# A limit on how far gathers run ahead that starts at three pairs and rises to eight

## The chip, the cores and the metric

The kernel runs on one core of one Trainium2 chip. The metric is the device time of a whole execution in microseconds (us), the median of several. The runs fell on at least three chips of the same type, and these do not behave alike. On two of them, numbers 13 and 5, the kernel before takes about 405 us; on chip 11 it takes about 358 us. Every comparison below is on one chip, beside runs of the kernel before on that chip, and within one call with one exception: of the eight runs of before that stand beside e9 to e12, seven are those of the call of e5 to e8, on the same chip. The first comparison of before and after has no chip number; it behaves like chip 13.

## The reference, cut to what matters

```python
B, S, N, D = (16, 4096, 2048, 512)
def reference(x, indices, w):
    gathered = x[np.arange(B)[:, None], indices, :].copy()   # B x N rows of 512 floats
    cs = np.cumsum(gathered, axis=1)
    return np.matmul(cs, w).astype(np.float32)
```

The rows to gather are sorted within a sequence, the running sum goes over the 2,048 gathered rows of each of 16 sequences, and the product with `w` makes 64 MB of output.

## The kernel before

Work goes in tiles of 128 rows, and two tiles make a pair `g`; there are 256 tiles and 128 pairs. GpSimd gathers a tile with an indirect DMA into one of eight pair buffers. TensorE (PE) sums a pair with matmuls against a triangular matrix (`sums`), VectorE adds the last column of the pair before (`carry`), PE multiplies by `w` (`project`), ScalarE copies the result out (`drain`) and SyncE's queue stores it. All order between engines is by hand-placed semaphores; `pool.need(s_a, n)` makes GpSimd wait until the sums of `n` pairs are done.

```python
NG = 16                                   # gather buffers in tiles: 8 pairs
NA = 2; NB = 2; NC = 4; NO = 8; AH = 2    # sums, products, carries, outputs; pairs that sums run ahead
# ... (buffers and semaphores cut)
def gather(t):
    g, r = divmod(t, R)                   # R = 2
    pool.need(s_a, g + 1 - NG // R)       # line 104: pair g waits for the sums of pair g - 8
    # ... (choice of the index column cut)
    nc.gpsimd.indirect_dma_start(out=g16[g % (NG // R)][:, r, :], ...).then_inc(s_g[t % NG], 16)

def sums(t):
    g, r = divmod(t, R)
    pe.need(s_g[t % NG], 16 * (t // NG + 1))
    pe.need(s_d, g - NA + 1)
    # ... four matmuls into pa[g % NA]; after the second tile: then_inc(s_a, 1)

def carry(g):
    dve.need(s_a, g + 1)
    # ... cst[g % NC] = pa[g % NA] + last column of the pair before; then_inc(s_d, 1)

# TensorE's order in the steady state:
for g in range(1, G - AH - 1):
    for j in range(R):
        sums(R * (g + AH) + j)
        project(g, j)
```

So one signal, the count `s_a` of summed pairs, wakes two engines: VectorE to carry, and GpSimd to gather further.

## Time and profile before

| | before |
|---|---|
| time, median of 3 | 404.81 us (404.65 to 404.89) |
| span of the profiled run | 403.2 us |
| busy: PE, weight loads, VectorE, ScalarE, GpSimd | 80, 45, 39, 33, 60% |
| queues' share of the 16 DMA engines: gathers, stores and loads | 58.2%, 44.2% |

No engine is full. The prediction below shows the table of windows, the queues and the start. One more reading: the timeline around 201 us, with start, length, engine, operation, and in brackets how long the engine had been idle and what released it.

```profile
201.26 0.39 PE L128 MATMUL pa<-ut,g 128*128 128x128 f16 x4
...
201.86 0.94 POOL L111 DMA_INDIRECT g<-in_x_dram,idxg  x1 [0.30 <-issue]
...
204.22 2.55 DVE L146 TENSOR_TENSOR cst<-pa,cst 128x1024 f16<-128x1024 f32 x2 [3.70 <-PE pa L128]
204.33 1.01 ACT L168 COPY ob<-pb 128x1024 f32<-128x1024 f32 x1 [3.11 <-remote]
204.46 0.94 POOL L111 DMA_INDIRECT g<-in_x_dram,idxg  x1 [1.66 <-PE pa L128]
```

The reader is to see one event. PE finishes the sums of a pair at 201.26 + 0.39 = 201.65 us. VectorE, which has been idle, starts the carry of that pair only at 204.22 us, 2.57 us later, and then does two pairs in one go. ScalarE, VectorE and GpSimd all wake within 0.24 us of each other. GpSimd's burst of gathers had ended at 201.86 + 0.94 = 202.80 us. I call this a **late signal**. It comes once in three pairs, about 1.4 us after a burst of six gathers: five starts 1.24 us apart, the last gather's 0.94 and GpSimd's pause of 1.66 us make 8.8 us, the period of three pairs.

### The profile page before, as it was taken

What the parts mean: (1) busy time and instruction counts of PE and PEld (TensorE: products, weight loads), DVE (VectorE), ACT (ScalarE), POOL (GpSimd) and SP (SyncE); (2) the same over time, 40 slices, a digit from 0 to 9 for tenths busy, and PEclk for the clock granted to TensorE, in tenths of its full rate; (3) what the DMA queues carried; (4) which work ended last, traced back from release to release, by engine and by line L of the source; (5) the groups of instructions that cost most, each with busy time, mean ns of one, the idle gap of its engine ahead of it and who ended that gap; (6) DMA issues with size and microseconds to landing.
All of it is one profiled execution on the core that took longest, in us unless ns stands there. A gap on an engine that the chain in (4) does not pass through costs nothing.

```text
span 403.2 us, 5096 instructions
## 1 busy us (share of the span) xinstructions
PE 324.4 (80%) x2064; PEld 182.4 (45%) x2064; DVE 159.2 (39%) x136; ACT 131.8 (33%) x132; POOL 241.6 (60%) x264
## 2 busy tenths in 40 slices
PE   5617988878888887888888788888878888888893
PEld 2303544444444444444444444444444444444451
DVE  2212443344444334434333443443344343433541
ACT  2102433333334333343333433343333333333442
POOL 6774666566666656666665666666566666666100
PEclk9867999999999999999999999999999999999998
DMA  7996999999999999999999999999999999999954
GB/s 175 140 128 111 278 262 262 280 272 270 259 283 257 272 269 269 279 255 284 256 275 264 278 268 266 277 258 271 267 278 271 257 284 264 277 251 281 287 227 191
DMA packets 56871, 102.32 MB, mean 254 GB/s; under 512 B 6800, under 2 KB 39824, under 8 KB 56848
## 3 DMA queue, kind: packets, MB, share of 16 engines
q0 software_dynamic: 36864, 33.57, 58.2%
q1 hardware_dynamic: 19712, 68.43, 44.2%
q8 instruction: 16, 0.26, 0.3%
q10 hardware_dynamic: 272, 0.00, 0.0%
q14 instruction: 7, 0.06, 0.0%
HBM read 68.42 MB, written 67.11 MB: 336 GB/s over the span
## 4 chain that ended last, share of the span: by engine, by line
PE 79%; issue 15%; DVE 2%; DMA 2%; ACT 0%; SPq 0%; ACTq 0%
PE pb L156 58%; PE pa L128 22%; DVE cst L146 2%; DMA g<-in_x_dram,idx_first 1%; DMA idx_first<-in_indices_dram 0%; ACT ob L168 0%; ACT ob L180 0%; ACTq L23 0%; SPq L332 0%; SPq L78 0%
## 5 line engine op out<-in xcount | busy, mean ns | idle before, releaser
L156 PE MATMUL pb<-w,cst 128*128 128x512 f16 x1024 | 266.7, 384 | 67.9 <-issue 56.6
L111 POOL DMA_INDIRECT g<-in_x_dram,idxg x252 | 236.4, 938 | 132.0 <-PE pa L128 66.3
L146 DVE TENSOR_TENSOR cst<-pa,cst 128x1024 f16<-128x1024 f32 x112 | 137.2, 1225 | 203.2 <-PE pa L128 144.8
L168 ACT COPY ob<-pb 128x1024 f32<-128x1024 f32 x127 | 128.5, 1012 | 261.9 <-remote 132.1
L156 PEld LDWEIGHTS pb<-w,cst 128*128 128x128 f16 x1024 | 94.1, 99 | 141.4 <-issue 65.8
L128 PE MATMUL pa<-ut,g 128*128 128x256 f16 (+1 forms) x1024 | 127.7, 248 | 4.3 <-DMA g<-in_x_dram,idx_first 2.7
L128 PEld LDWEIGHTS pa<-ut,g 128*128 128x128 f16 x1024 | 89.8, 99 | 69.4 <-issue 7.8
L142 DVE CAST cst<-pa 128x1024 f16<-128x1024 f32 x16 | 19.5, 1222 | 25.6 <-PE pa L128 18.4
L244 PE MATMUL pb<-zeros 128*128 128x512 f16 x14 | 5.2, 535 | 1.5 <-DVE zeros L248 1.5
L111 POOL DMA_INDIRECT g<-in_x_dram,idx_first x4 | 3.9, 986 | 2.0 <-DMA idx_first<-in_indices_dram 1.1
L244 PEld LDWEIGHTS pb<-zeros 128*128 128x128 f16 x14 | 1.7, 131 | 3.8 <-issue 1.9
L302 ACT CAST w<-w 128x512 f16<-128x512 f32 x2 | 1.2, 618 | 2.8 <-DMA w<-in_w_dram 2.8
L265 DVE CAST w<-w 128x512 f16<-128x512 f32 x2 | 0.9, 452 | 3.1 <-DMA w<-in_w_dram 3.1
L251 DVE CAST idxf<-idx 128x128 f32<-128x128 uint32 x2 | 0.5, 238 | 3.5 <-DMA idx<-in_indices_dram 3.5
L299 ACT ACT_TABLE_LOAD x1 | 1.3, 1283 | 1.5 <-SPq L78 1.5
L180 DVE COPY ob<-pb 128x512 f32<-128x512 f32 x1 | 0.7, 691 | 2.1 <-PE pb L156 2.1
L180 ACT COPY ob<-pb 128x512 f32<-128x512 f32 x1 | 0.6, 586 | 0.7 <-PE pb L156 0.7
L248 DVE MEMSET zeros<- 128x256 uint32 x1 | 0.3, 272 | 1.1 <-SPq L78 1.1
L256 PEld LDWEIGHTS pb<-ident,idxf 128*128 128x128 f32 x2 | 0.4, 187 | 0.6 <-DVE idxf L251 0.3
L262 DVE CAST idxg<-pb 128x128 uint32<-128x128 f32 x2 | 0.5, 292 | 0.2 <-PE pb L256 0.2
L256 PE MATMUL pb<-ident,idxf 128*128 128x128 f32 x2 | 0.5, 303 | 0.0
L215 POOL MEMSET ident<- 128x128 f32 x1 | 0.2, 205 | 0.5 <-SPq L78 0.5
(8 smaller groups left out, 1.6 us busy)
## 6 DMA issues: line engine op xcount, KB each, us to landing
out_dram<-ob SPq DMA_DIRECT2D x127, 512.0 KB
g<-in_x_dram,idxg POOLq DMA_INDIRECT x252
w<-in_w_dram SPq DMA_DIRECT2D x4, 256.0 KB
out_dram<-ob SPq DMA_DIRECT2D x2, 256.0 KB, 2.7
idx<-in_indices_dram SPq DMA_DIRECT2D x2, 128.0 KB, 2.6
g<-in_x_dram,idx_first POOLq DMA_INDIRECT x4
idx_first<-in_indices_dram ACTq DMA_DIRECT2D x1, 2.0 KB, 2.2
idx_first<-in_indices_dram SPq DMA_DIRECT2D x1, 2.0 KB, 2.0
```

The lines of the kernel that those rows point to most:

```text
L111: nc.gpsimd.indirect_dma_start(out=g16[g % (NG // R)][:, r, :], out_offset=None, in_=x_flat, in_offset=bass.IndirectOffsetOnAxis(ap=ap, ax ...
L128: mm = nc.tensor.matmul(out=pa[g % NA][:, c] if r == 0 else pa[g % NA][:, c, :, Q:], lhsT=g16[g % (NG // R)][:, r, c * P : (c + 1) * P], r ...
L142: nc.vector.tensor_copy(out=dst[:], in_=pa[g % NA][:]).then_inc(s_d, 1)
L146: nc.vector.tensor_tensor(out=dst[:], in0=pa[g % NA][:], in1=last.unsqueeze(2).broadcast_to([P, DC, R, P]), op=mybir.AluOpType.add,).then_ ...
L156: mm = nc.tensor.matmul(out=pb[g % NB][:, j], lhsT=cst[g % NC][:, c, j, :], rhs=w16[:, c, :], start=(c == 0), stop=(c == DC - 1),)
L168: nc.scalar.copy(out=ob[g % NO][:], in_=pb[g % NB][:]).then_inc(s_e, 1)
L180: copy(out=ob[g % NO][:, j], in_=pb[g % NB][:, j]).then_inc(s_el[j], 1)
L244: nc.tensor.matmul(out=pb[NB - 1][:, R - 1], lhsT=zeros[:, :P], rhs=zeros[:], start=True, stop=True)
L256: nc.tensor.transpose(out=pb[k % NB][:, 0, :P], in_=idxf[:, k, :], identity=ident[:]).then_inc(s_pt, 1)
L265: nc.vector.tensor_copy(out=w16[:, c, :], in_=w32[:, c, :]).then_inc(s_wc, 1)
L299: nc.scalar.copy(out=spare[:], in_=zeros[:, :1])
L302: nc.scalar.copy(out=w16[:, c, :], in_=w32[:, c, :]).then_inc(s_wc, 1)
```

## The change

The intent is to keep GpSimd from running eight pairs ahead in the start, where VectorE, PE and ScalarE stood still while it did, and to reach the old lead of eight by pair 80.

```diff
     NG = 16
+    EARLY = 3
+    RAMP = 16
     NA = 2
...
     def gather(t):
         g, r = divmod(t, R)
-        pool.need(s_a, g + 1 - NG // R)
+        pool.need(s_a, g + 1 - min(NG // R, EARLY + g // RAMP))
```

Pairs 0 to 15 may run 3 pairs ahead of the sums, pairs 16 to 31 may run 4, and so on to 8 from pair 80. I call this limit the **lead**, and the time from the end of the last gather to the end of the kernel the **tail**.

## The prediction

> **What bounds the kernel now.** I read the page first. TensorE (PE) is 80% busy, no engine is full, but the DMA row of the slices stands at 9 from the seventh slice to the thirty-eighth. Then I cut the span into stretches, because a mean over a start, a steady state and an end says little. This is the table of windows (columns: stretch, its length, busy us of PE, weight loads, VectorE, ScalarE and GpSimd with instruction counts, granted clock, DMA share, GB/s):
>
> ```profile
> 10.00:20.00 10.00, 7.03 (x42) 3.77 (x40) 2.58 (x3) 1.01 (x1) 7.56 (x9) 0.83 0.90 137
> 20.00:30.00 10.00, 1.48 (x4) 0.59 (x5) 1.23 (x1) 0.00 (x0) 7.56 (x9) 0.61 0.91 132
> 30.00:40.00 10.00, 7.42 (x31) 3.57 (x30) 2.58 (x3) 2.02 (x2) 4.25 (x5) 0.70 0.61 109
> 40.00:100.00 60.00, 51.00 (x336) 29.17 (x333) 25.50 (x21) 21.25 (x21) 38.46 (x41) 1.00 1.09 269
> 100.00:376.00 276.00, 230.88 (x1507) 131.63 (x1508) 115.54 (x95) 95.13 (x94) 176.74 (x189) 1.00 1.09 270
> ```
>
> The reader is to see two different kernels here. From 40 to 376 us the DMA share is the same 1.09 in both stretches (1.08 to 1.09 in finer cuts) (above 1 because packets of two queues overlap in time), at 269 GB/s: I take that for its ceiling. From 10 to 40 us it moves half as much, and PE nearly stands still from 20 to 30 us.
>
> Next the DMA part of the page, for what one pair of sequence tiles costs the transfer engines:
>
> ```profile
> q0 software_dynamic: 36864, 33.57, 58.2%
> q1 hardware_dynamic: 19712, 68.43, 44.2%
> ```
>
> Of 403.2 us, 58.2% is 234.7 us of gathers, 1.83 us for each of 128 pairs; 44.2% is 178.2 us, nearly all stores, 1.39 us a pair. Together 3.2 us, and divided by the share of 1.09 that runs, 2.95 us. The chain in order of time has a period of three pairs, which is the same rate:
>
> ```profile
> 204.03 1.47 issue
> 205.50 1.04 PE pb L156 x4
> ...
> 212.84 1.47 issue
> 214.30 1.04 PE pb L156 x4
> ```
>
> 212.84 - 204.03 = 8.81 us for three pairs, 2.94 us each. PE alone would take 2.4 us a pair: in the unbroken parts of the same chain two groups of four projections (0.86 us each) and two groups of four sums (0.44 and 0.22) make one pair. So in the steady state the transfers' full engines and the pace agree, although no instruction is shown waiting for a gather there.
>
> Last, the start, in the timeline and in the waits of 10 to 40 us:
>
> ```profile
> 16.73 1.23 DVE L146 TENSOR_TENSOR cst<-pa,cst 128x1024 f16<-128x1024 f32 x1 [4.78 <-PE pa L128]
> 27.24 1.23 DVE L146 TENSOR_TENSOR cst<-pa,cst 128x1024 f16<-128x1024 f32 x1 [9.29 <-remote]
> 28.52 1.89 PE L156 MATMUL pb<-w,cst 128*128 128x512 f16 x4 [8.74 <-issue]
> 34.37 1.01 ACT L168 COPY ob<-pb 128x1024 f32<-128x1024 f32 x1 [17.28 <-remote]
> 34.55 0.94 POOL L111 DMA_INDIRECT g<-in_x_dram,idxg  x1 [4.05 <-PE pa L128]
> ```
>
> After the carry of the second pair at 16.73, VectorE idles 9.29 us, PE 8.74, and ScalarE 17.28 between the first and the second result. GpSimd meanwhile issues a gather every 1.24 us without a pause from 3.26 to 30.5 us and stops only because it is eight pairs ahead. The sums that the carry at 27.24 waits for are recorded as done by 16.93 us. **What holds their signal back for ten microseconds no view says**; it is not an unlanded gather of that pair, and the long delays stop when GpSimd stops: after the last gather (376 us) no such gap is left in the timeline.
>
> **What the Trainium skill says.** "DMA: Bandwidth & Descriptors", section "Issuing engines are not separate DMA queues", says that transfers of all issuers run on the same 16 DMA engines and interleave; the trace agrees, the two queues together fill 1.08 of them. The same page, "Queues, rings and completion order", says that each engine takes turns between its queues packet by packet, so gathers ahead of need delay a store by their share and not by their whole backlog; no view of the kernel before shows that directly. "Perfetto Trace Analysis", section "DMA Instruction — SWDGE (GPSIMD)", says that the end of such an instruction is the end of descriptor generation; agreed, the first gather is issued at 3.26 and 1.13 us long, but the chain holds 5.82 us until PE can use it. "TensorE: Matmul & The Clock Gate", section "Why this matters for your kernels", says that idle gaps over some 3 us drop the clock; agreed, the clock is 0.61 from 20 to 30 us.
>
> **The change part by part.** Nothing is removed or added in work: 256 gathers of 0.94 us, the same matmuls, copies and stores; the comparison of orders shows only waits on GpSimd, one from the fourth pair on instead of the ninth.
>
> *Start.* Pair 3 may go when pair 0 is summed (10.7 us; it went at 10.91, no change). Pair 4 now waits for the sums of pair 1, about 16.7 us instead of 13.40. Then each pair waits for the sums three pairs back. If the long holdup belongs to the uninterrupted stream of gathers, it goes, and PE can walk on from 20 us. What that is worth is bounded by the transfers: between 10 and 40 us the DMA share lost against 1.08 is (0.18 + 0.17 + 0.47) / 1.08 x 10 = 7.6 us; counted in work, three stores were issued where the steady pace makes ten, 7 x 1.39 = 9.7 us. Against that, the pause of GpSimd between about 13 and 16.7 us leaves the engines partly idle, at most 2 to 3 us. **Estimate for the start: 6 to 9 us less.**
>
> *Pairs 4 to 80, three to seven ahead.* Does a lead of three suffice? From the sums of a pair to those three later: wake 0.3, second gather 1.25, landing as long as the first gather's 5.8, the sums 0.4: 7.8 us, 2.6 us a pair, less than the 2.94 that the transfers take. With the 2.6 us delay that one pair in three shows in the steady state it would be about 8.6 us when shared over the three, still just under 8.8. So 0 to 3 us may be lost in the first sixteen pairs, nothing from four ahead.
>
> *Steady state from pair 80 and end.* Same lead, same full engines: no change. But if PE stays on the heels of the gathers, fewer pairs are left when they end: from 376 us on the share is 0.64, over 27 us, and each pair less in that tail saves about half a microsecond, 0 to 4 us.
>
> Sum: -7.5 + 1 - 2 = about -8.5 to -9.5 us, **395.5 us**.
>
> **The rivals.** (1) *The holdup is not the gathers' doing.* One store and PE's throttled clock are in the same window. For it: signals are late in the steady state too. Then the start is unchanged and gathers only start later: 403 to 406 us. (2) *The lead is too short and PE waits for gathers.* For it: gathers share full engines and then land later than 5.8 us; at 7.5 us the loop is 9.5 us, 0.2 us a pair over sixteen pairs, 3 us, and a late signal now stalls GpSimd and then PE. Against it: the ramp gives a fourth pair after sixteen. Alone +3 to +8 us: 408 to 412. (3) *Hidden anyway:* if transfers are the only limit, a lead changes when bytes move, not how many; then only the lost 7.6 to 9.7 us can come back and 394 is the floor. (4) *The late signals vanish over the whole ramp* and the end shortens: 385 to 390. The ceiling of 1.08 speaks against more.
>
> **Range and chances.** Start repaired, rest the same (half): 393 to 399. Start repaired and a shorter tail (15%): 386 to 392. Little or nothing (28%): 399 to 405. Starved (7%): above 406. The 2% line is 396.7 us, in the midst of the likeliest case. Hence 395.5 us, range 387 to 405; faster 0.52, within 2% 0.42, slower 0.06.
>
> **What the profile after would show.** Right: VectorE's 9.29 and ScalarE's 17.28 us idle times gone, PE's gap of 8.74 us gone, the clock not at 0.61 from 20 to 30 us, five or more stores by 40 us, then 1.08 share and the period of 8.8 us again. GpSimd's wait for PE grows early and costs nothing. Wrong: the same gaps at 17 to 34 us (rival 1), PE or its weight loads waiting for gathers between 20 and 70 us with a DMA share below 1.0 (rival 2), or a period below 8.8 us, which would say that the share of 1.08 was no ceiling and that the gain is larger than told.

## The result, and the profile after

| | before | after |
|---|---|---|
| time, median of 4 | 404.85 us (404.65 to 405.32) | 407.59 us (406.86 to 407.75) |
| span of the profiled run | 403.2 us | 406.0 us |
| end of the last gather | 376.51 us | 379.39 us |
| from there to the end (the tail) | 26.7 us | 26.7 us |

The ratio is 1.0062, with a 95% interval of 1.0045 to 1.008. A ratio here is always the mean time of one kernel's fast runs over that of the other's of the same rounds, so it is not quite the ratio of the medians quoted. The profile after is of its slowest run, 407.75 us. The change is within 2%, on the slow side, and outside the range of the prediction.

The start is repaired as foreseen. This is the table of windows of the kernel after (stretch, its length, busy us and instruction counts of PE, weight loads, VectorE, ScalarE and GpSimd, granted clock, DMA share, GB/s), and below it three lines of its timeline:

```profile
10.00:20.00 10.00, 7.68 (x40) 3.92 (x41) 4.20 (x4) 1.01 (x1) 4.31 (x5) 0.66 0.56 85
20.00:30.00 10.00, 7.05 (x46) 3.57 (x45) 3.44 (x4) 2.86 (x3) 6.29 (x7) 1.00 1.03 214
30.00:40.00 10.00, 8.88 (x59) 4.54 (x57) 4.00 (x4) 3.21 (x4) 6.54 (x8) 1.00 1.04 241
```

```profile
17.32 1.01 ACT L170 COPY ob<-pb 128x1024 f32<-128x1024 f32 x1 [10.37 <-PE pb L158]
17.54 2.55 DVE L148 TENSOR_TENSOR cst<-pa,cst 128x1024 f16<-128x1024 f32 x2 [4.82 <-PE pa L130]
17.78 0.94 POOL L113 DMA_INDIRECT g<-in_x_dram,idxg  x1 [3.87 <-PE pa L130]
```

From 20 to 30 us PE is busy 7.05 us where it was 1.48, at full clock where it was 0.61. ScalarE has 8 copies in these 30 us where it had 3. VectorE's longest idle time here is 4.82 us instead of 9.29. But the first row shows the price: GpSimd is busy only 4.31 us of the ten, and the DMA share is 0.56 at 85 GB/s where the kernel before had 0.90 at 137. The last timeline line tells why: GpSimd stood for 3.87 us, until the signal of PE's sums woke it at 17.78 us.

Now compare how far the engines get by one moment. These are windows of the kernel before, then of the kernel after, cut at 12, 260 and 376 us. An instruction that lies across a cut counts in both rows.

```profile
12.00:260.00 248.00, 200.41 (x1279) 113.39 (x1280) 97.61 (x80) 79.62 (x79) 158.88 (x170) 0.97 1.05 253
260.00:376.00 116.00, 96.88 (x634) 55.12 (x633) 48.45 (x40) 39.80 (x40) 74.15 (x80) 1.00 1.09 270
376.00:406.00 30.00, 20.74 (x130) 11.36 (x128) 9.72 (x9) 9.69 (x10) 0.51 (x1) 0.93 0.58 208
```

```profile
12.00:260.00 248.00, 204.61 (x1268) 111.91 (x1268) 96.45 (x80) 78.09 (x78) 157.39 (x169) 0.96 1.05 250
260.00:376.00 116.00, 97.27 (x635) 55.46 (x636) 48.62 (x40) 40.31 (x40) 75.02 (x80) 1.00 1.09 271
376.00:406.00 30.00, 22.17 (x139) 12.04 (x137) 11.62 (x10) 10.71 (x11) 1.87 (x2) 1.00 0.68 234
```

By 260 us both kernels have done 80 instructions of VectorE, nearly all of them carries, and the kernel after has one gather fewer, 169 against 170. So the start's lead of some 9 us (the carry of pair 20 starts at 73.8 us instead of 82.4, counting VectorE's carries in order) is gone by then. At 376 us the kernel after has ten instructions of VectorE and two gathers left, the kernel before nine and one.

Where it goes is seen at the steps of the ramp. This is the timeline of the kernel after where the lead goes from 4 to 5 (pair 32):

```profile
107.28 1.01 ACT L170 COPY ob<-pb 128x1024 f32<-128x1024 f32 x1 [5.15 <-remote]
107.74 0.94 POOL L113 DMA_INDIRECT g<-in_x_dram,idxg  x1 [0.30 <-issue]
...
110.82 1.23 DVE L148 TENSOR_TENSOR cst<-pa,cst 128x1024 f16<-128x1024 f32 x1 [4.50 <-PE pa L130]
...
111.06 0.93 POOL L113 DMA_INDIRECT g<-in_x_dram,idxg  x1 [2.39 <-PE pa L130]
```

Given one more pair at once, GpSimd issues ten gathers without a pause from 96.55 to 108.68 us, instead of six. The signals in this stretch are later still: ScalarE has been idle 5.15 us before it wakes at 107.28, VectorE 4.50 us before 110.82. Two more rows end the argument, GpSimd's last gather in the kernel before and in the kernel after:

```profile
375.57 0.94 POOL L111 DMA_INDIRECT g<-in_x_dram,idxg  x1 [0.30 <-issue]
```

```profile
378.45 0.94 POOL L113 DMA_INDIRECT g<-in_x_dram,idxg  x1 [0.30 <-issue]
```

The last gather starts 2.88 us later, and the span is longer by as much. What follows the last gather takes the same time in both.

### The profile page after: what moved, and what is told of

It reads as the page before. It is cut to its first block, busy times and chain, and to the rows that moved or that the text cites. A ratio compares the mean times of both kernels' runs of the same rounds, so it can differ in the third digit from the quotient of the medians.

```text
span 406.0 us, 5095 instructions
## 1 busy us (share of the span) xinstructions
PE 331.5 (82%) x2064; PEld 182.3 (45%) x2064; DVE 159.5 (39%) x136; ACT 131.8 (32%) x132; POOL 241.7 (60%) x264
## 4 chain that ended last, share of the span: by engine, by line
PE 71%; issue 13%; DMA 6%; POOL 4%; DVE 3%; another core or an unknown queue 1%; SPq 1%; ACT 0%; ACTq 0%
PE pb L158 51%; PE pa L130 20%; DMA g<-in_x_dram,idxg 5%; POOL g L113 4%; DVE cst L148 2%; DMA w<-in_w_dram 1%; DVE cst L144 1%; DVE w L267 0%; SPq L203 0%; SPq L207 0%; ACT ob L182 0%; SPq L195 0%; SPq L334 0%; ACTq L23 0%
## 5 line engine op out<-in xcount | busy, mean ns | idle before, releaser
L130 PE MATMUL pa<-ut,g 128*128 128x256 f16 (+1 forms) x1024 | 130.3, 250 | 19.4 <-issue 11.3
L130 PEld LDWEIGHTS pa<-ut,g 128*128 128x128 f16 x1024 | 88.8, 99 | 90.8 <-issue 26.5
```

Of the source, the lines that this page charges most:

```text
L130: mm = nc.tensor.matmul(out=pa[g % NA][:, c] if r == 0 else pa[g % NA][:, c, :, Q:], lhsT=g16[g % (NG // R)][:, r, c * P : (c + 1) * P], r ...
```

## The experiments

Theory A, in its final form: **on this chip the stream of gathers keeps one timetable whatever the lead, and the time is the end of that stream plus a tail that grows with the lead.** A smaller lead in the start makes the sums earlier against the same gathers; that is not progress, it is gathers not yet issued, and it is paid back when the lead rises. Only the lead at the end can shorten the kernel. Rival B: the repaired start is a real gain, and the change lost it by something of its own, a lead of three that is too short or a ramp that slows the middle. Rival C: the transfers' full engines are the ceiling, as the prediction took them to be.

A grew. Before e1 to e4 it said "paid back", with rival C's full engines as what sets the pace; the tail of 2.4 us for each pair of lead was read from these four runs, and e13 and e17 are its tests on a slower chip.

All edits are of line 104 unless shown otherwise. Labels that end in "slow" or "third" name the hope for a chip of that kind, not the chip that the run got.

### Constant leads and a quick ramp (one call, chip 13, before 404.99 us)

```diff
-        pool.need(s_a, g + 1 - NG // R)
+        pool.need(s_a, g + 1 - 3)                        # e1_lead3
+        pool.need(s_a, g + 1 - 4)                        # e2_lead4
+        pool.need(s_a, g + 1 - 6)                        # e3_lead6
+        pool.need(s_a, g + 1 - min(NG // R, 3 + g // 2)) # e4_fast_ramp
```

e1_lead3, expected: 

> Lead of 3 pairs to the end, no ramp. Theory (paid back: the transfers' full engines set the pace, the 8.8 us that the changed kernel is ahead at pair 27 are the gathers it has not yet issued, and each step of the ramp pays for one pair of them and loses a little more in a long holdup): with no step nothing is paid back, and the end has five pairs fewer to finish after the last gather; 393 to 399 us, and the sums at pair 77 come 5 us or more before those of the kernel before. Rival (starved: three pairs are too short a lead, TensorE waits for gathers that have not landed): slower than the changed kernel, 412 us or more, with waits for gathers all along and a DMA share below 1.0.

e2_lead4, expected: 

> Lead of 4 pairs to the end. Theory paid back: 394 to 400 us, one pair more to finish at the end than with 3. Rival starved: better than with 3, still no faster than 405 us. Both allow that 4 is better than 3 if 3 starves a little.

e3_lead6, expected: 

> Lead of 6 pairs to the end. Theory paid back: between 4 and 8 pairs, 398 to 403 us, as two pairs fewer are left at the end (some half a microsecond each) and three pairs fewer are gathered in the start. Rival starved: 404 to 405 us, as the kernel before, because six pairs are enough.

e4_fast_ramp, expected: 

> From 3 pairs to 8 within ten pairs of sums. Theory paid back: the lead is paid for in the start, at once and while the engines still have room, with no steps later; 401 to 405 us, the start's gain kept in part. Rival starved: the short lead lasts only for the first pairs, so 404 to 406 us. This run tells the cost of the late steps: about 3 to 6 us less than the changed kernel if the steps cost, the same as the changed kernel if only the start does.

| kernel | time, us | ratio to before (95%) | last gather ends | from there to the end |
|---|---|---|---|---|
| before (lead 8), the first profile | 404.85 | | 376.51 | 26.7 |
| e1, lead 3 | 404.79 median, scattered 401.71 to 413.43 | 0.9996 (0.9955 to 1.0036) | 382.88 | 17.1 |
| e2, lead 4 | 396.07 | 0.9778 (0.9761 to 0.9794) | 377.53 | 17.1 |
| e3, lead 6 | 400.5 | 0.9888 (0.9872 to 0.9905) | 376.96 | 21.9 |
| e4, 3 to 8 by pair 10 | 405.11 | 1.0004 (0.9987 to 1.0021) | 376.76 | 26.7 |

One run of e1, at 413.43 us, was slow (over 1.5% above the kernel's fastest) and is not in its ratio. The times of e2 and e3 lie in the ranges of the theory; that of e1 lies in neither range, and that of e4 in the rival's, just outside the theory's. The two columns on the right are of the profiled runs. The last gather ends at 377 us, give or take 0.6, for leads of 4, 6 and 8, and the tail is 17.1, 21.9 and 26.7 us. That is (26.7 - 17.1) / 4 = 2.4 us for each pair of lead, the pace of PE alone in the prediction's chain: the pairs gathered but not summed when gathering ends are summed afterwards, at PE's own pace (7, 5 and 3 pairs of sums end after the last gather with leads of 8, 6 and 4, most of them 2.39 us apart). The windows of the lead of 4, and its last gather:

```profile
12.00:260.00 248.00, 208.29 (x1343) 117.07 (x1341) 101.36 (x83) 82.99 (x82) 158.54 (x169) 0.99 1.07 261
260.00:376.00 116.00, 96.79 (x630) 54.07 (x628) 48.46 (x40) 40.24 (x40) 73.83 (x79) 1.00 1.09 268
376.00:406.00 30.00, 11.82 (x68) 6.07 (x68) 5.93 (x6) 5.89 (x7) 1.23 (x2) 0.93 0.44 151
```

```profile
376.59 0.94 POOL L111 DMA_INDIRECT g<-in_x_dram,idxg  x1 [0.30 <-issue]
```

By 260 us it has 83 instructions of VectorE, three more than the kernel before, on one gather fewer. After 376 us 6 are left instead of 9. So its sums are three pairs closer to the gathers, and they stay so to the end because the lead never rises.

A lead of three is too short. In the waits of e1 (what waited for what, us in total, times, longest):

```profile
PEld pa L128 <- DMA g<-in_x_dram,idxg: 85.5, 100, 2.3
```

PE's weight loads wait for gathers to land a hundred times, where the same list of the kernel before has one wait for a gather, that for the first pair. The profile is of e1's fastest run, 401.71 us; even there the last gather ends 6.4 us later than that of before, and the tail is no shorter than with four. The late signals are nearly gone in it: by the count described below it has 3 late carries, where the kernel before has 37. So their going does not make this kernel faster, since PE now waits for gathers. This is the part of rival B that holds, for a constant lead of three. The quick ramp is at lead 8 by pair 10, repairs nothing (the carry of pair 3 starts at 34.3 us, as before), and equals the kernel before.

### Ramps at the other end, half stores, a pause between gathers (one call, chip 11, before 357.99 us)

```diff
+        pool.need(s_a, g + 1 - max(4, min(NG // R, 4 + (G - 1 - g) // 8)))   # e5_fall: 8, falling to 4
+        pool.need(s_a, g + 1 - min(NG // R, 4 + max(0, (g - 88) // 8)))      # e6_rise: 4, rising to 8
```
```diff
# e7_half_stores: wrong on purpose, half of the output is not written
-        nc.sync.dma_start(out=dst, in_=ob[g % NO][:]).then_inc(s_o[g % NO], 16)
+        nc.sync.dma_start(out=dst[:, 0], in_=ob[g % NO][:, 0]).then_inc(s_o[g % NO], 16)
# e8_paced: after each gather from the fifth on, 0.2 us of other work for GpSimd (the lines that make pad and s_pad, and the if, cut)
+            pool.need(s_pad, t - FIRST)
+            nc.gpsimd.memset(pad[:], 0.0).then_inc(s_pad, 1)
```

e5_fall, expected: 

> Lead 8 until pair 95, then one pair less every 8 pairs, 4 at the last: the start of the kernel before, the end of lead 4. Theory (the end: from the end of the last gather the kernel needs 7.5 us and 2.39 us for each pair of lead, so 17.1 us at 4 and 26.7 at 8; the last gather is at 377 us in all constant leads because the full engines bring it there): the end shrinks by 9.6 us, but the last gather comes later by the four stores that must now be out before it, 4 x 1.39 = 5.6 us: about 401 us, last gather at 382, tail 17. Rival (it is the start alone that makes lead 4 faster, by the holdup of 17 us that it avoids): 405 us, nothing gained at the end.

e6_rise, expected: 

> Lead 4 until pair 95, then one pair more every 8 pairs, 8 at the last: the start of lead 4, the end of the kernel before. Theory: 27 us from the last gather to the end again, so the 9 us of lead 4 are lost for the most part: 402 to 406 us, the sums at pair 84 still 9 us ahead of the kernel before and at pair 119 no more than 3. Rival (start alone): 396 to 398 us.

e7_half_stores, expected: 

> Kernel before, each store writes one of its two rows per partition: half of the result is missing on purpose, the arithmetic is whole. Theory (full transfer engines set the pace of 2.93 us a pair): stores cost 0.7 us a pair instead of 1.39, so 2.5 us a pair by share, 2.3 in time, below the 2.49 that GpSimd needs to issue two gathers: 2.5 us a pair, 345 to 360 us. Rival (late signals of TensorE are tied to gathers issued without pause and set the pace by themselves): the period stays near 8.8 us for three pairs, 400 to 405 us.

e8_paced, expected: 

> Kernel before with a 0.2 us memset on GpSimd after each gather, so that gathers no longer come without pause. If uninterrupted gathers cause the late signals: the 2.57 us waits of VectorE become fewer or shorter and the 17 us of ScalarE in the start shrink; if full engines set the pace, the time is the same within 1% all the same (402 to 408 us), the last gather near 377 us and 27 us from there. If the signals themselves set the pace, it gets faster with them gone: below 395 us. If GpSimd is slowed so far that it becomes the bound, 2 x 1.45 = 2.9 us a pair, also about 405 us, but with a DMA share below 1.05.

Measured: 358.47 us (1.0013), 360.4 (1.0081), 338.83 (0.9466) and 363.82 (1.0158). These numbers don't test the theories as written, because the call fell on another chip, where the kernel before itself is 47 us faster. No late signal is found in any trace of this chip: among pairs 4 to 124 no carry starts more than 1.5 us after both its sums and the carry before are done, where the kernel before on the slower chip has 37 such carries.

### The same on chip 11 with the changed kernel and the lead of four (before 357.92 us)

e9_after_again, expected: 

> The changed kernel once more, beside the others on one chip. The second set of runs fell on a chip where the kernel before takes 358 us and shows none of the late signals; the first on one where it takes 405. Slow kind of chip: 1.004 to 1.009 of the kernel before, as on record. Fast kind: GpSimd's 2.49 us a pair is the bound there and TensorE waits for gathers, so a short lead at first costs only what it starves: 1.00 to 1.02.

e10_lead4_again, expected: 

> Lead 4 to the end. Slow kind of chip: 0.976 to 0.980 again. Fast kind: no backlog of pairs stands behind the last gather there, so the tail has nothing to give: 0.99 to 1.02 of the kernel before.

e11_fall_again, expected: 

> Lead 8 falling to 4 over the last 32 pairs. On a slow chip, theory (time = last gather + 7.5 us + 2.39 us for each pair of lead at the end): tail 17 us instead of 26.7, last gather 0 to 6 us later than 376.5, so 395 to 402 us in all, faster than the kernel before by 1 to 2.4%. Rival (what lead 4 gains comes from the start): 404 to 406 us. On a fast chip: the same as before, as measured (1.001).

e12_rise_again, expected: 

> Lead 4 rising to 8 over the last 32 pairs. On a slow chip, theory: the 9 us that it is ahead at pair 84 are given back by pair 119, tail 26.7 us, 402 to 407 us in all. Rival (start): 396 to 398 us. On a fast chip: 1.008 of the kernel before, as measured.

Measured: the changed kernel 362.54 us, 1.0137 (1.0111 to 1.0163); lead 4, 358.67 us, 1.0031; fall, 358.37 us, 1.001; rise, 358.72 us, 1.0028. The rise is the kernel of e6, which had 1.0081 a call earlier, so differences of half a per cent between calls mean nothing here. The lead of four in the waits, and in the table of windows from 40 to 320 us:

```profile
PEld pa L128 <- DMA g<-in_x_dram,idxg: 71.5, 135, 2.5
```

```profile
40.00:320.00 280.00, 266.76 (x1702) 140.22 (x1700) 129.97 (x107) 107.27 (x106) 199.43 (x213) 1.00 1.13 299
```

Here PE waits for gathers to land, 135 times, and the engines carry 299 GB/s at a share of 1.13. The lead hardly matters on this chip: with four the last gather ends at 338.3 us and the kernel's span at 356.8, with the changed kernel at 329.8 and 358.8. The gathers move with the lead and the end does not, the reverse of chip 13. The changed kernel's loss is there early: the carry of pair 20 starts 3.5 us later than with lead 4 (67.13 against 63.65 us), and the span ends 2.0 us later in this profile, which is of its fastest run. That the start at three is the reason is likely, but no run shows it on this chip.

### The falling lead on the slower chip (chip 13, before 404.96 us)

e13_fall_slow, expected: 

> Lead 8 falling to 4 over the last 32 pairs, a third time, for a chip with late signals (kernel before near 405 us). Theory (time = last gather + 7.5 us + 2.39 us for each pair of lead at the end): tail 17 us instead of 26.7, last gather 0 to 6 us later than 376.5: 395 to 402 us. Rival (what lead 4 gains comes from the start): 404 to 406 us. If the chip is again one without late signals (kernel before near 358 us), 0.999 to 1.004 of the kernel before, and nothing is decided.

Measured: 398.14 us (397.46 to 399.2), 0.9837 (0.9814 to 0.986). This kernel has the start of before, unrepaired (the carry of pair 3 starts at 34.4 us), and only its lead over the last 32 pairs is smaller. Its last gather ends at 378.44 us, 1.9 us later than that of before, and 17.3 us follow, where theory A foretold 17. So the span is 1.9 us longer before that point and 9.4 us shorter after it (395.7 against 403.2); rival B foretold no gain. Its windows show the carries catching up while the lead falls, 44 instructions of VectorE where before has 40:

```profile
260.00:376.00 116.00, 103.44 (x684) 59.45 (x682) 53.61 (x44) 43.57 (x44) 73.15 (x78) 1.00 1.10 283
376.00:406.00 30.00, 13.20 (x79) 6.68 (x77) 5.67 (x6) 6.60 (x7) 1.88 (x2) 0.97 0.49 161
```

**Most of the gain of the lead of four is had here with the bad start left in place.**

### The rising lead, half stores and the pause, meant for the slower chip (chip 11 again, before 358.36 us)

e14_rise_slow, expected: 

> Lead 4 up to pair 88, then one pair more every 8 pairs up to 8: the good start of the constant lead of 4 with the end of the kernel before. On a chip where the kernel before takes about 405 us: theory (the start's gain is only gathers not yet issued, and is paid back as the lead grows; the time is the end of the last gather plus a tail of about 26.7 us at lead 8): 402 to 407 us, some 9 us ahead of the kernel before at pair 84, nothing or little ahead at pair 119, and 26 to 27 us from the end of the last gather to the end of the kernel. Rival (a repaired start is kept, and the ramp of the change lost it only because it began at 3 or because it rose early): 396 to 398 us, still some 8 us ahead at pair 119.

e15_half_slow, expected: 

> Wrong on purpose: the store of a pair writes only the first half of its bytes, all else is as in the kernel before. On a chip where the kernel before takes about 405 us: if the bytes of the DMA engines set the pace of the steady stretch, 340 to 360 us, as on the other chip, and the DMA share falls below 1.0. If the late signals (sums done, VectorE starting some 2.6 us after them, at every third pair) set the pace by themselves: 395 to 405 us, with three pairs still taking 8.6 to 8.8 us.

e16_paced_slow, expected: 

> A small memset of GpSimd (some 0.2 us) between the gathers of the steady stretch, so that gathers do not follow each other without pause. On a chip where the kernel before takes about 405 us: if gathers issued back to back are what makes the signals late, the late signals shrink or go, and the time is below 395 us where they set the pace, or about 403 to 407 us where the transfers do. If the late signals have another cause: they stay as they are, and the time is 404 to 412 us.

Measured: 358.91 us (1.002), 339.09 (0.9462) and 363.91 (1.0155), the numbers of e12, e7 and e8 again. One row is used below, the windows of the half stores on this chip:

```profile
40.00:320.00 280.00, 273.61 (x1807) 154.35 (x1806) 137.76 (x114) 114.36 (x113) 211.33 (x226) 1.00 1.06 212
```

### The rising lead and the half stores on a slower chip (chip 5, before 405.22 us)

e17_rise_third, expected: 

> The kernel of e14 again, because e14 fell on the fast chip and so told nothing of the question. On a chip where the kernel before takes about 405 us: theory (the start's gain is only gathers not yet issued, and is paid back as the lead grows): 402 to 407 us, with 26 to 27 us from the end of the last gather to the end of the kernel. Rival (a repaired start is kept, and the ramp of the change lost it only because it began at 3 or rose early): 396 to 398 us.

e18_half_third, expected: 

> The kernel of e15 again, wrong on purpose (half of each store). On a chip where the kernel before takes about 405 us: if the bytes of the DMA engines set the pace of the steady stretch, 340 to 360 us and a DMA share below 1.0. If the late signals set the pace by themselves: 395 to 405 us, with three pairs still taking 8.6 to 8.8 us.

e17 measured 405.52 us (404.81 to 405.96), 1.0011 (0.9994 to 1.0028). Its windows:

```profile
12.00:260.00 248.00, 208.50 (x1344) 116.82 (x1344) 101.38 (x83) 82.99 (x82) 158.86 (x170) 0.99 1.07 261
260.00:376.00 116.00, 93.37 (x569) 51.21 (x569) 44.66 (x37) 36.43 (x36) 74.75 (x80) 0.94 1.06 253
376.00:406.00 30.00, 20.68 (x130) 11.33 (x128) 9.70 (x9) 9.69 (x10) 0.45 (x1) 0.93 0.59 210
```

By 260 us it stands where the lead of four stands, 83 instructions of VectorE. From 260 to 376 us, while its lead rises to eight, it does 80 gathers like the kernels before and after but only 37 instructions of VectorE, where these do 40; and then 9 are left, as in the kernel before. The carry of pair 84 starts 9.1 us ahead of before (260.5 against 269.6 us) and that of pair 119 is level (374.0 against 374.1). **So a good start, kept for two thirds of the kernel and far beyond any lead of three, is worth nothing if the lead is eight at the end.** With e13 that decides between A and B on the slower chips.

e18 measured 404.39 us (two runs), 0.998 (0.996 to 1.0). With half the bytes of the stores its windows are:

```profile
40.00:100.00 60.00, 50.74 (x334) 29.00 (x333) 25.03 (x22) 21.25 (x21) 38.22 (x42) 1.00 0.96 182
100.00:376.00 276.00, 230.55 (x1508) 131.42 (x1506) 115.43 (x95) 95.13 (x94) 176.76 (x189) 1.00 0.95 180
```

The rate falls from 270 to 180 GB/s and the share from 1.09 to 0.95, and the pace does not move: 95 instructions of VectorE and 189 of GpSimd from 100 to 376 us, the same counts as before, and in its timeline the late signals come 8.75 us apart (204.10 and 212.85 us). On chip 11 the same program gains 5.4%, with GpSimd 75% busy (211.33 of 280 us). So rival C is out on the slower chips: the bytes of the stores do not set the pace there.

### The gathers, counted

Counting the rows of GpSimd in the timelines gives the end of the n-th gather (us), on the slower chips:

| gather | before | after | e1, lead 3 | e2, lead 4 | e4, quick ramp | e17, rising |
|---|---|---|---|---|---|---|
| 9th | 14.34 | 18.71 | 17.46 | 14.26 | 14.54 | 14.51 |
| 25th | 37.97 | 41.54 | 40.74 | 38.04 | 37.91 | 37.96 |
| 97th | 143.89 | 146.28 | 148.28 | 143.60 | 143.34 | 143.52 |
| 181st | 266.88 | 269.64 | 272.81 | 266.87 | 267.03 | 266.66 |
| 256th | 376.51 | 379.39 | 382.88 | 377.53 | 376.76 | 376.45 |

This is the shortest form of theory A. From the 25th on, whatever the lead, bad start or good, the gathers keep one timetable to about a microsecond, except where the start lets only three pairs ahead for long. (The falling lead of e13, not in the table, delays its last gathers, by 1.9 us at the end.) The changed kernel falls 4.4 us behind that timetable at its 9th gather, is 3.6 us behind at the 25th, and 2.4 to 2.9 behind to the end. The steps of its ramp delay the sums, not the gathers. Between gathers 25 and 256 it needs 337.8 us and the kernel before 338.5. The table shows that the timetable does not move with the lead; it does not show that GpSimd sets it by itself, for GpSimd waits once in six gathers for a signal of PE (the 1.66 us above).

## Why the prediction was wrong

**Right in mechanism and size, as sums are counted.** The holdup in the start went with the unbroken stream of gathers, as told. "Estimate for the start: 6 to 9 us less" was met at pair 27: its sums end 8.8 us earlier (93.8 against 102.6 us). The signs that the prediction named for a repaired start are there, but "GpSimd's wait for PE grows early and costs nothing" is half wrong: it grew, and the gathers stayed late. Half of a sign for starvation is there too: between 20 and 70 us PE's weight loads waited for gathers nine times, 8.4 us in all, though at a DMA share of 1.05 and not below 1.0.

**The step that failed first is the sum itself:** it carried those 6 to 9 us to the end. It counted the start in stores and in DMA share lost, as if the kernel's end followed from the sums. On this chip the end follows from the gathers, and in the start the kernel before loses no gathers: its 25th ends at 37.97 us, that of the lead of four at 38.04. e17 shows it best, with 9.1 us at pair 84 and none at pair 119. Beside that, the terms of the sum make -8.5 us, or 396.3 us; the 395.5 us takes the far end of "-8.5 to -9.5". (The DMA row of the page stands at 9 from the fifth slice on, not the seventh; nothing rests on that.)

**"0 to 4 us" for the tail** was mis-sized at the root. The tail is 26.7 us before and after, because it depends on the lead at the end, which the change leaves at eight. It is 2.4 us for each pair of lead, not "about half a microsecond", so e2 and e13 get 9.4 to 9.6 us from it. The prediction had the right quantity in hand, pairs left when the gathers end, and the wrong reason for it to change: PE cannot stay on the heels of gathers that are allowed to run eight pairs away.

**The pause of GpSimd, "at most 2 to 3 us",** is near in size to what survived: the gathers are 2.9 us late at the end, and that is the whole slowdown. But it was set down as engines partly idle, a small deduction from a gain that did not last, and not as a delay of the stream that the end follows.

**"0 to 3 us may be lost in the first sixteen pairs, nothing from four ahead."** The last part holds for the gathers (e2, and the steps of the ramp), not for the sums: each step makes the signals later for a while (4.50 and 5.15 us instead of 3.7 and 3.1), and in these stretches the earlier sums are given back.

**"I take that for its ceiling"**, of a share of 1.09 at 269 GB/s, was wrong. e18 moves 180 GB/s at the same pace, and chip 11, though another chip, reaches 1.13 at 299 GB/s with a program that differs only in its lead. A busy share that stays flat beside a steady pace can be the consequence of the pace. Rival 3 gave 394 us as a floor from this ceiling; the lead of four came to 396.1, but for another reason, the tail.

**What stays open.** Why PE's signals come late on chips 13 and 5 and never on chip 11, and what fixes the timetable of the gathers. The late signals are part of the pace: in the chain that the prediction shows, PE works some 7.3 of the 8.81 us of three pairs and stands still for 1.47, until the carry that starts late at 204.22 us is done. That most of them come about 1.4 us after a burst of gathers ends suggests that issuing gathers holds them back, but this is argued and not shown: the run that would have told (a pause between gathers, e8 and again e16) fell twice on the chip that has no late signals. The record speaks on both sides. On the slower chip the holdup of the start grows with the lead: the carry of pair 3 starts at 19.4, 23.1, 28.7 and 34.3 us with leads of 3, 4, 6 and 8. But on chip 11, e5 issues 182 gathers without a pause, from 3.35 to 229.75 us, and not one late carry is found. So gathers issued back to back are not enough by themselves. Of the change's 2.9 us, that they arise in the start is shown by the counts; that GpSimd's 3.87 us wait is their cause is read from its timeline, and is supported by e4, e2 and e17, which do not have that wait and are not late at the 25th gather. Some of the 4.4 us at the 9th is not that wait: in this profile the first sums start 0.45 us later than before (9.97 against 9.52), and the seventh gather, which waits for them, 0.8 us later (11.73 against 10.91).

The best version measured is the constant lead of four, 0.9778 on chip 13; on chip 11 it is 1.0031, the same.

## What to carry to other kernels

Before a start is repaired, find the stream whose end sets the kernel's end, and ask whether the start delays that stream; here eight microseconds of idle engines delayed only the consumers, who had a backlog to work off in any case. A producer that is far ahead when it finishes leaves that many items as a tail at the consumer's pace, so where the consumer ends the full lead behind, the smallest lead that does not starve it is best, most of all at the end: four, of the leads 3, 4, 6 and 8 tried on chip 13. On chip 11, where PE waited for gathers, a lead of 4 took 1.0031 of the time of 8. A flat DMA share is not a ceiling until a run with fewer bytes has become faster.

## What the Trainium skill lacked or had wrong

- "Perfetto Trace Analysis", section "Tensor Engine Instruction (MATMUL, LD_WEIGHTS)", has the propagation of the semaphore update as a last stage after the modelled end of a matmul, without a duration. On chips 13 and 5 that stage, or something the trace doesn't separate from it, took about 2.5 us once in three pairs (2.57 us at 201.65 us in the kernel before); on chip 11 no such delay was seen. No page that I found tells of signals held up in step with another engine's gathers.
- No page that I found says that chips of one type can differ this much for one program: 404.99 and 405.22 us on two chips, 357.99 us on a third. With half the bytes of the stores it was 404.39 us on one and 339.09 us on another.
- "DMA: Bandwidth & Descriptors", section "Issuing engines are not separate DMA queues", is not contradicted by any run here. The step from a flat busy share of 1.09 to a ceiling was the prediction's own: the same gathers ran with 0.95 at the same pace once the stores were halved, and a share of 1.13 at 299 GB/s was reached on another chip.
